# The S5 blocks' small products moved behind the dense slots of the step before, in a hybrid decoder block

## The chip, the core and the metric

The kernel runs on one core of a Trainium2 chip. The metric is the device time of one execution in microseconds; the kernel before takes 861.79 us, the median of three runs from 861.11 to 861.98. The engines are named as in the profile: PE is the tensor engine and PEld its weight loads, DVE the vector engine, ACT the scalar engine, POOL the GpSimd engine, which here only issues DMAs in the part that matters, and SP the queue that issues most loads. A product's result goes to one of eight PSUM buffers, from which DVE or ACT must copy or use it before the buffer can serve again.

## The reference

One decoder layer on 512 tokens of width 1024, with 16 meta tokens ahead of them, everything in float32. After a norm and one wide input projection, two token mixers run side by side. Then come gates, an output projection, and an MLP with squared ReLU; the change lies in the mixers.

```
# GLA: four heads, chunked linear attention with decay
scores  = where(mask, q_in @ k_in.T, 0);   o_intra = scores @ v
o_inter = q_inter @ state
state   = decay_chunk * state + k_state.T @ v
# S5: 64 groups of 16 channels, 64 complex states each
x_t = Lbar x_{t-1} + Bbar u_t ;  y_t = Re(C x_t) + D u_t
g_s = gelu(y);  glu = g_s @ w_glu + b_glu
```

## The kernel before, in words

**Dense slots.** The wide projections are cut into column blocks of 128. The list `dense` holds them in order, each with a function that takes the finished weights; `slot()` (line 761) fetches the weights of the next two entries and runs the next entry, 24 products of up to 512 columns with a split into a high and a low part (`feat_tile`, three products for each of eight depth tiles). Weights come through SP; ACT makes the high part (`whi`, line 164), DVE the low part (`wlo`, line 179), each with three buffers, so a new split starts as a slot ends. A slot takes about 5.4 us of PE. Between slots the code places the small products of the two mixers, on plain float32 operands. These places are what the change rearranges.

**Order.** In the whole stage `pinned[0]` is true: PE runs strictly in program order. ACT, DVE, POOL and SP are ordered by a planner, which takes the earliest written instruction among those that it reckons ready; after that each engine keeps to its list and waits at the head of it. In `first_block` DVE and ACT keep program order too.

**PSUM.** Four buffers (`ps_mm`, line 110) serve the dense slots, four (`ps_sm`, line 111) all the small products. `bank()` gives one of the latter; a fifth in a row waits until an earlier one has been read out.

**GLA heads** (class `Head`, line 953). `scores` (line 1054) makes products on 64 columns of the array and copies them under the causal mask into `sc` with two predicated copies on DVE (lines 1064 and 1065). `states` (line 1067) makes four states in two buffers: state 0 from the meta tokens (`kmeta`, `vmeta`, which `turn_keys` prepares with casts on ACT and subtractions on DVE), the others from `ktok` and `vtok`. `outputs`, `turn_outputs`, `turn_values` and `turn_keys` are the other places of a head; the `turn_` functions are full-width transposes.

**S5 blocks** (class `Block`, line 1110). Eight blocks of eight groups. For each block:

- `loads` fetches B and lam; `tables` (line 1124, a generator with four parts) makes M2 (lines 1130 to 1138) and M1 (lines 1140 to 1144) on DVE; `turns` (line 1147) makes the table E and loads U, eight transfers.
- `kernels` (line 1160): the kernel rows, products on 32 columns (in the profile `M,BA`), copied to `krow` and stored to `kpad`; `kernel_loads` (line 1173) reads them back shifted, eight transfers, as M3.
- `scan` (line 1180, a generator with three parts): the inputs (`U,M`, two buffers), multiplied by E on DVE and exchanged by ACT; then the scan along the chunks; then the states X.
- `output` (line 1211): the S5 output in one buffer (`M,U` and `M,X`), followed by a gelu: a square on ACT (line 1226), DVE (line 1227), a sigmoid on ACT (line 1228) and DVE (line 1230, `qt`).
- `turn_output` (line 1232): four transposes, a copy, and four stores to `qd`, from where the glu stage at the end of this part reads all blocks but the last (lines 1448 and 1450, `qi`, `gh`, `gl`).

**The steps.** `first_block` does head 0 and block 0. The loop that follows does step b for b from 1 to 7, with block b, and with head b while b is below 4. A step has five dense slots (step 7 has three): behind the first, head 0's transposes (step 2 alone), then kernel rows and inputs of block b and output of block b-1; behind the second, the outputs of the head before; behind the third, transposes of values; behind the fourth, transposes of keys and of the outputs of the head before; behind the fifth, scores and states, and last the transposes of block b-1's S5 output. Step 1 makes its inputs behind the second slot. Steps 1 to 3 hold a head's slots, step 4 four gate slots and the first r slot, step 5 five r slots, step 6 two r slots and others. Each r slot (`r_slot`, line 1252) gives DVE three more operations (lines 1260 to 1263), the first of which wait for a load of the gated head outputs (`ro`).

## Time and profile before

| what | value |
|---|---|
| median of the runs | 861.79 us (861.11 to 861.98) |
| profiled execution, its own time | 861.4 us |
| its span | 859.7 us |
| mean granted clock of PE | 0.997 |
| matmul instructions | 4952 |
| ACT whi, 128x1024 | 81 of 1059 ns |
| DVE wlo, 128x1024 | 81 of 1225 ns |
| M3 loads (M from kpad), landing | 64, 64 KB each, 2.6 us |

The profile is that of one execution. Rows of a timeline hold start and duration in microseconds, the engine, the line, the operation, the tiles written and read, the size, and how many such rows follow each other; a bracket gives the idle time of that engine before the row, and what ended it. Line 61 is the helper through which all products go, line 66 that of the transposes, so these rows are told apart by their tiles. Products on plain float32 operands are two rows each. A product row's duration holds time in which the next one runs already, so the distance between starts is what counts. In `first_block`, rows of DVE and ACT stand under line 79.

### The profile page before, as it was taken

Reading aid. Unit: us, or ns where it says so; the run is one execution under the profiler, and the core shown is the slowest. Engines: PE = TensorE matmul, PEld = TensorE weight load, DVE = VectorE, ACT = ScalarE, POOL = GpSimd, SP = SyncE. Lnnn points to the kernel's source line nnn. Section 1 sums busy time; section 2 is a strip of 40 time slices with the busy share of each in tenths; the row PEclk is TensorE's granted clock in tenths of the full one; section 3 lists DMA queues with packets and bytes.
Section 4 is the critical chain, followed back from the end, with each engine's and each line's share of the span. In section 5 each row is a group of like instructions: output and inputs, shape, how many; then the busy total and the mean of one; then the engine's idle time right before and its main releaser. Section 6 shows DMA issues by size and latency. Waiting matters only on the chain.

```text
span 859.7 us, 13744 instructions
## 1 busy us (share of the span) xinstructions
PE 849.5 (99%) x4952; PEld 726.6 (85%) x4952; DVE 680.2 (79%) x1264; ACT 465.0 (54%) x816; POOL 151.1 (18%) x265
## 2 busy tenths in 40 slices
PE   9999999999999999999999999999999999999996
PEld 8998899898988888888888889988888888888885
DVE  6999889988787499856888788667666777688886
ACT  7677466676764455335454466433222246885763
POOL 1123120140303222341121421011121100000001
PEclk9999999999999999999999999999999999999998
DMA  9887775566465856977788896498989967866564
GB/s 313 194 281 225 224 143 146 147 174 168 115 156 154 241 156 149 257 202 270 233 271 266 270 294 196 147 323 291 360 262 343 352 223 234 278 195 196 172 199 144
DMA packets 172491, 192.66 MB, mean 224 GB/s; under 512 B 18648, under 2 KB 127352, under 8 KB 172424
## 3 DMA queue, kind: packets, MB, share of 16 engines
q1 hardware_dynamic: 145040, 109.66, 45.1%
q0 software_dynamic: 25408, 77.93, 27.2%
q10 hardware_dynamic: 1976, 4.20, 1.6%
q8 instruction: 39, 0.64, 0.3%
q14 instruction: 28, 0.23, 0.1%
HBM read 149.52 MB, written 42.24 MB: 223 GB/s over the span
## 4 chain that ended last, share of the span: by engine, by line
PE 52%; issue 2%; POOL 1%; DMA 1%; DVE 1%; ACT 0%; DVEq 0%; POOLq 0%
PE mm L61 36%; PE sm L61 16%; DMA qi<-qd 1%; POOL M L1178 0%; PE sm L66 0%; POOL td L1277 0%; DVE c L1964 0%; POOL qd L1250 0%; DVE c L1938 0%; POOL qi L1448 0%; DVE gl L1450 0%; DVEq L2040 0%; ACT gh L164 0%; DMA kpad<-krow 0%; DVE ff_r L150 0%
## 5 line engine op out<-in xcount | busy, mean ns | idle before, releaser
L164 ACT ACTIVATE whi<-wraw 128x1024 fp32r<-128x1024 f32 x81 | 85.8, 1059 | 181.1 <-PE mm L61 177.6
L179 DVE TENSOR_TENSOR wlo<-wraw,whi 128x1024 fp32r<-128x1024 f32 x81 | 99.1, 1225 | 79.0 <-ACT whi L164 77.2
L61 PE MATMUL mm<-xh,whi 128*128 128x512 f32 (+2 forms) x464 | 158.5, 342 | 0.0
L61 PE MATMUL mm<-xh,wlo 128*128 128x512 f32 (+2 forms) x464 | 155.5, 335 | 0.0
L61 PE MATMUL mm<-xl,whi 128*128 128x512 f32 (+2 forms) x464 | 155.4, 335 | 0.0
L61 PE MATMUL mm<-hh,whi 128*128 128x512 f32 (+1 forms) x272 | 100.9, 371 | 0.0
L61 PE MATMUL mm<-hl,whi 128*128 128x512 f32 (+1 forms) x272 | 100.8, 371 | 0.0
L61 PE MATMUL mm<-hh,wlo 128*128 128x512 f32 (+1 forms) x272 | 100.8, 371 | 0.0
L61 PEld LDWEIGHTS mm<-xh,whi 128*128 128x128 f32 x464 | 87.4, 188 | 9.7 <-issue 1.0
L61 PEld LDWEIGHTS mm<-xh,wlo 128*128 128x128 f32 x464 | 87.4, 188 | 9.0
L61 PEld LDWEIGHTS mm<-xl,whi 128*128 128x128 f32 x464 | 87.4, 188 | 8.4
L1881 DVE TENSOR_TENSOR wlo<-wraw,whi 128x1024 fp32r<-128x1024 f32 x56 | 68.4, 1223 | 21.4 <-ACT whi L1877 21.3
L61 PE MATMUL sm<-wlo,fh 128*128 128x512 f32 x192 | 74.9, 390 | 0.0
L61 PE MATMUL sm<-whi,fl 128*128 128x512 f32 x192 | 74.8, 390 | 0.0
L61 PE MATMUL sm<-whi,fh 128*128 128x512 f32 x192 | 74.8, 389 | 0.0
L1877 ACT ACTIVATE whi<-wraw 128x1024 fp32r<-128x1024 f32 x56 | 58.7, 1050 | 15.5 <-PE mm L61 11.7
L61 PEld LDWEIGHTS mm<-hh,whi 128*128 128x128 f32 x272 | 51.3, 189 | 8.8
L61 PEld LDWEIGHTS mm<-hh,wlo 128*128 128x128 f32 x272 | 51.3, 189 | 8.7
L61 PEld LDWEIGHTS mm<-hl,whi 128*128 128x128 f32 x272 | 51.3, 189 | 8.6
L164 ACT ACTIVATE fh<-f 128x512 fp32r<-128x512 f32 x48 | 30.2, 629 | 36.8 <-PE sm L61 23.0
L61 PE MATMUL mm<-gl,whi 128*128 128x512 f32 x128 | 50.0, 390 | 0.1
L61 PE MATMUL mm<-gh,whi 128*128 128x512 f32 x128 | 49.9, 390 | 0.0
(490 smaller groups left out, 1863.2 us busy)
## 6 DMA issues: line engine op xcount, KB each, us to landing
wraw<-in_w_ff_dram SPq DMA_DIRECT2D x56, 512.0 KB, 7.5
wraw<-in_w_in_dram SPq DMA_DIRECT2D x46, 512.0 KB, 5.6
w2raw<-in_w_ff_dram POOLq DMA_DIRECT2D x16, 1024.0 KB, 9.0
t2d<-w2t POOLq DMA_DIRECT2D x16, 1024.0 KB, 6.3
wraw<-t2d SPq DMA_DIRECT2D x32, 512.0 KB, 4.2
wraw<-in_w_glu_dram SPq DMA_DIRECT2D x16, 512.0 KB, 5.2
M<-kpad POOLq DMA_DIRECT2D x64, 64.0 KB, 2.6
wraw<-in_w_o_gla_dram SPq DMA_DIRECT2D x8, 512.0 KB, 7.4
```

What stands on the lines that cost most here:

```text
L61: ins = nc.tensor.matmul(*args, **kw)
L164: return S.activation(dst, src, AF.Copy, scale=scale)
L179: V.tensor_sub(lo, raw, f32(hi))
L1877: halved = S.activation(bh, raw, AF.Copy)
L1881: V.tensor_sub(bl, raw, f32(bh))
```

## The change

The diff leaves `first_block` and the work itself as they are. It changes where the pieces stand.

- In `states`, the second product of each pair is made first, so the meta state is second.
- From block 2 on, kernel rows and inputs of block b+1 and the output of block b stand at the end of step b: in steps 1 to 3 between scores and states, from step 4 on by themselves. The kernel loads of block b+1 follow there.
- The transposes of a block's S5 output stand behind the first slot of the next step, one slot after that output; those of block 0 behind the third slot of step 1.
- Loads of B and lam come behind the first slot, tables start there too (two parts stand ahead of the fifth slot), and turns of the next block stand ahead of the fourth slot.
- Step 1 keeps kernel rows of block 1, the output of block 0 and the inputs of block 1 where they were.
- Block 7's output stands at the end of step 7, and its transposes one slot later; both come one dense slot earlier than before.

```diff
--- before.py
+++ after.py
@@ -1068,7 +1068,7 @@
             self.st = []
             for t in range(0, TT, 2):
                 pst = bank().rearrange("p (t v) -> p t v", t=2)
-                for i in range(t, t + 2):
+                for i in (t + 1, t):
                     k, v = (self.ktok[:, i - 1, :], self.vtok[:, i - 1, :]) if i else (self.kmeta, self.vmeta)
                     PE.matmul(pst[:, i % 2], k, v, start=True, stop=True)
                 for i in range(t, t + 2):
@@ -1348,29 +1348,34 @@
             continue
         this = heads[b] if b < HEADS else None
         last = heads[b - 1] if 0 < b <= HEADS else None
+        after = blocks[b + 1] if b + 1 < NBLK else None
         if b == 1:
             with tc.issue_after(heads[0].held.ins):
                 list(blk.turns())
-        following = iter(())
-        if b + 1 < NBLK:
-            following = blocks[b + 1].tables()
+        following = after.tables() if after else iter(())
         slot()
-        if b == 2:
-            heads[0].turn_outputs()
-        blk.kernels()
-        steps = blk.scan()
-        if b > 1:
+        if b == 1:
+            blk.kernels()
+            steps = blk.scan()
+            blocks[0].output()
+            blk.kernel_loads()
+        else:
+            blocks[b - 1].turn_output()
+            if b == 2:
+                heads[0].turn_outputs()
             next(steps)
-        blocks[b - 1].output()
-        blk.kernel_loads()
+            if after:
+                after.loads()
         if this:
             this.decay_load()
             with tc.issue_after(this.taken.ins), tc.issue_after(heads[0].held.ins):
                 list(this.decays())
+        if b > 1:
+            next(following, None)
         slot()
         list(steps)
-        if b + 1 < NBLK:
-            blocks[b + 1].loads()
+        if b == 1:
+            after.loads()
         if last:
             last.outputs()
         if this:
@@ -1381,14 +1386,16 @@
             slot()
         if this:
             this.turn_values()
+        if b == 1:
+            blocks[0].turn_output()
         next(following, None)
+        if after:
+            list(after.turns())
         slot()
         if this:
             this.turn_keys()
         if last and b > 1:
             last.turn_outputs()
-        if b + 1 < NBLK:
-            list(blocks[b + 1].turns())
         if b == HEADS:
             sgb.close()
             sg.close()
@@ -1396,16 +1403,21 @@
             po_ = pool("po", stack=so, padded=True)
             ogh = mk(po_, [P, KT, SEQ], F32R, tag="ogh")
             ogl = mk(po_, [P, KT, SEQ], F32R, tag="ogl")
-        next(following, None)
-        if b < NBLK - 1:
+        for _ in range(2):
+            next(following, None)
+        if after:
             slot()
         if this:
             this.scores()
+        if after:
+            after.kernels()
+            steps = after.scan()
+            next(steps)
+        blk.output()
+        if after:
+            after.kernel_loads()
+        if this:
             this.states()
-        blocks[b - 1].turn_output()
-        next(following, None)
-    slot()
-    blocks[-1].output()
     slot()
     blocks[-1].turn_output(last=True)
     while at[0] < len(dense):
```

## The prediction

> **What bounds the kernel now.** I read the first part of the page, then the waits of PE, then a table of windows over the attention and S5 stage, and then the PE rows around the places where small products stand between the dense slots.

> ```profile
> span 859.7 us, 13744 instructions
> PE 849.5 (99%) x4952; PEld 726.6 (85%) x4952; DVE 680.2 (79%) x1264; ACT 465.0 (54%) x816; POOL 151.1 (18%) x265
> ```

> ```profile
> PE sm L61 <- DVE xss L517: 1.3, 1, 1.3
> ```

> PE works from end to end: its longest wait is 1.3 us, at the start. The change adds and removes no product, only reorders them, so it can gain only what PE loses at the seams between kinds of work and in short waits that a busy PE hides. It can lose whatever PE waits for in a new place. The reserve on the other engines differs by stretch (columns of the table: stretch, its length, then busy time and instructions of PE, PEld, DVE, ACT, POOL, granted clock, DMA share, GB/s):

> ```profile
> 284.00:297.60 13.60, 13.60 (x67) 11.18 (x65) 3.79 (x5) 4.72 (x7) 4.61 (x8) 1.00 0.95 282
> 297.60:329.00 31.40, 31.40 (x205) 25.91 (x204) 29.93 (x51) 15.86 (x28) 7.19 (x13) 1.00 0.63 179
> 329.00:360.00 31.00, 30.96 (x202) 25.70 (x202) 30.28 (x50) 14.13 (x24) 7.51 (x14) 1.00 0.81 197
> ```

> At the end of step 4 (284 to 297.6) DVE is busy 3.79 of 13.6 us. In steps 5 and 6 it is busy 29.93 of 31.4 and 30.28 of 31: it is full there, and what PE wants from it earlier, it gets late.

> **Seams on PE.** Step 7's S5 place stands between two dense slots of 512 columns:

> ```profile
> 360.28 0.39 PE L61 MATMUL mm<-ogl,whi 128*128 128x512 f32 x1
> 360.50 0.39 PE L61 MATMUL mm<-ogh,wlo 128*128 128x512 f32 x1
> 360.82 0.66 PE L61 MATMUL sm<-M,BA 128*32 128x128 f32 x16
> 361.42 1.15 PE L61 MATMUL sm<-U,M 128*64 128x65 f32 x32
> 362.40 0.39 PE L61 MATMUL sm<-M,U 128*64 128x128 f32 x4
> ...
> 363.93 0.39 PE L61 MATMUL sm<-M,X 128*64 128x128 f32 x4
> 364.25 0.50 PE L61 MATMUL mm<-ogh,whi 128*128 128x512 f32 x1
> 364.59 0.40 PE L61 MATMUL mm<-ogl,whi 128*128 128x512 f32 x1
> ```

> A row starts as soon as the one before lets it, so starts are read, not durations. A dense product holds PE for 0.22 us (360.28 to 360.50). Kernel rows take 361.42 - 360.82 = 0.60, inputs 0.98, four output rows (363.93 - 362.40)/7 = 0.22, all eight groups of them 1.75. Into the place the gap is 0.32, so 0.10 is lost; the last output rows are followed after 0.32 in place of 0.22, 0.10 lost; the next gap is 0.34, 0.12 lost. So a place of products on 64 or 32 columns of the array costs 0.32 us beside its work, 0.10 on the way in and 0.22 on the way out. A place of full-width transposes loses less:

> ```profile
> 354.80 0.60 PE L66 MATMUL sm<-ident,qt 128*128 128x128 f32 x4
> 355.16 0.48 PE L61 MATMUL mm<-ogh,whi 128*128 128x512 f32 x1
> 355.47 0.40 PE L61 MATMUL mm<-ogl,whi 128*128 128x512 f32 x1
> ```

> Four transposes take 0.36, and the gap behind the next product is 0.31, 0.09 lost.

> The change joins scores and the S5 place in steps 1 to 3 (the S5 places of steps 2 to 4 go there). Each joining drops one way in and one way out, 0.32, and adds a seam from scores (64 columns) to kernel rows (32 columns), which no row shows. Its bounds are 0 and the 0.22 of a way out; I take 0.10, the way in, since that too begins narrow products. So 0.22 is saved per step, 0.7 in all (0.3 to 1.0). From step 4 on the S5 place only moves from behind the first slot to behind the last. The transposes of blocks 1 to 3, behind the states today, now stand behind the first slot: between 0 and 0.09 more each, since the states' end costs something too; I take 0.1 in all. Net gain at the seams 0.6 us.

> [...]

> **The meta state second.** In the first block the meta product waits for its operands from DVE:

> ```profile
> 130.91 0.71 DVE L79 TENSOR_TENSOR meta<-sm,meta 16x256 fp32r<-16x256 f32 x2
> 131.33 0.28 PE L61 MATMUL sm<-e_fq,e_fk 128*64 128x64 f32 x2
> 131.76 0.36 PE L61 MATMUL sm<-meta 80*128 80x256 f32 x1 [0.16 <-PE sm L61]
> ```

> ```profile
> 213.35 0.28 PE L61 MATMUL sm<-e_fq,e_fk 128*64 128x64 f32 x2
> 213.56 0.38 PE L61 MATMUL sm<-meta 80*128 80x256 f32 x1
> 213.78 1.46 PE L61 MATMUL sm<-vtok,ktok 128*128 128x256 f32 x6
> ```

> DVE ends at 131.62. From the last scores to meta it is 0.43 us, in step 2 (second fence) 0.21. So 0.22 is lost, and another state in front covers it: two of the six vtok,ktok rows, a third of 1.46. Gain 0.2; in step 2 there is no such wait, and there the swap costs nothing.

> **The last output.** Block 7's output and its transposes come one dense slot earlier, block 6's transposes two. Their way through DRAM ends just too late now:

> ```profile
> 398.82 0.39 PE L61 MATMUL mm<-gh,whi 128*128 128x512 f32 x1
> 399.27 0.50 PE L61 MATMUL mm<-gl,whi 128*128 128x512 f32 x1
> ```

> 0.45 in place of 0.22: 0.2 us lost, which the 5 us of lead removes. Behind it no row shows anything late; the dense work goes on. Gain 0.2.

> **Banks, the new wait.** The small products share four PSUM buffers (line 111). Today only step 2's first place uses more, six, with head 0's transposes ahead of S5:

> ```profile
> 180.86 1.23 PE L61 MATMUL sm<-U,M 128*64 128x65 f32 x32
> 181.97 0.44 PE L61 MATMUL sm<-M,U 128*64 128x128 f32 x4
> 182.24 0.39 PE L61 MATMUL sm<-M,X 128*64 128x128 f32 x4
> ```

> Inputs take 1.11 there in place of 0.98 and the first output rows 0.27 in place of 0.22, so 0.2 us is lost, and that goes with the change, since the place then holds three buffers of transposes alone. But the joined place uses seven: scores 1, kernel rows 1, inputs 2, output 1, states 2. So the output waits until the scores are copied out, and everything behind it on PE, states and the next dense slot, waits too.

> ```profile
> 213.46 1.22 DVE L179 TENSOR_TENSOR wlo<-wraw,whi 128x1024 fp32r<-128x1024 f32 x1 [3.56 <-ACT whi L164]
> 214.60 0.73 DVE L1064 COPY_PREDICATED sc<-tri,sm 64x512 f32<-64x512 int32 x1
> 215.35 0.45 DVE L1065 COPY_PREDICATED sc<-tri,sm 64x256 f32<-64x256 int32 x1
> ```

> ```profile
> 171.55 0.38 PE L61 MATMUL sm<-meta 80*128 80x256 f32 x1
> 174.68 0.45 DVE L1065 COPY_PREDICATED sc<-tri,sm 64x256 f32<-64x256 int32 x1
> ```

> DVE starts a weight split (wlo) as ACT finishes its part, 0.1 us before the scores are done, and the two copies follow it. In step 2 the buffer is free at 215.35 + 0.45 = 215.80; the output wants it when scores, kernel rows and inputs are through, 213.56 + 0.60 + 0.98 = 215.14. PE waits 0.65 us, and I take the same for step 3, whose pattern is the same. In step 1 DVE is behind: 174.68 + 0.45 = 175.13 against 171.55 + 1.58 = 173.13, 2.0 us; block 2's tables and turns, now due for this place, cannot fall behind the copies, work of later steps can. I take 1.2, between step 2's 0.65 and 2.0 and nearer the first, since that queue is the usual one. Sum 2.5 us (2.0 to 3.3). The states' two buffers are those of kernel rows and first inputs; their copies follow the scores' by under 1 us, while the output products take 1.75, which hides them. If DVE is later than that, it costs so much again.

> [...]

> **Covered moves.** Loads of B and lam, the eight U loads, kernel row stores and the eight M3 loads move on SP's and POOL's queues with their blocks; kernel loads keep a whole step (about 31 us) before use, U gains, since output frees its buffer a slot earlier. Nothing if the order within the queues holds; DMA share is already 0.95 in 284 to 297.6, so a late weight there could cost PE some tenths. Sigmoids of S5 now stand beside those of the gate slot, which drops table loads on ACT; PE does not wait for ACT there, so 0.

> **Sum.** -0.6 at the seams, -0.2 for meta, -0.2 for the last output, -0.2 in step 2's first place, +2.5 for the banks: +1.3 us. The profiled execution took 861.4 (span 859.7 and 1.7 around it), the median is 861.8; I carry the difference over: 861.8 + 1.3 = 863.1.

> **Rivals.**

> (a) *DVE's full stretch makes PE wait, slower.* Block 6's inputs need its table, and turned outputs need the gelu chain.

> ```profile
> 297.62 0.69 DVE L1261 TENSOR_TENSOR rs<-rs,ro 128x512 f32<-128x512 f32 x1 [3.02 <-DMA ro<-og]
> 300.83 0.39 PE L61 MATMUL sm<-M,X 128*64 128x128 f32 x4
> 306.23 0.69 DVE L1230 TENSOR_TENSOR qt<-q,sm 128x512 f32<-128x512 f32 x1 [0.46 <-ACT q L1228]
> 329.32 0.70 DVE L1144 TENSOR_TENSOR M<-M,B 128x512 f32<-128x512 f32 x1
> 329.70 0.88 PE L61 MATMUL sm<-U,M 128*64 128x65 f32 x12
> ```

> The chain from output to qt took 306.92 - 301.05 = 5.9 us in step 5. Today four slots cover it; then one slot, 24 x 0.22 to 0.23, 5.4. Block 6's table ends at 330.02, 0.3 after its inputs start; it falls due a slot earlier. DVE also stands 3.02 us for a load that S5 work queued behind it shares. For it: the full DVE rows. Against: S5 work of block 5 moves into the idle stretch before 297.6 and eases what follows, and PE's own waits give time back. It decides once DVE is more than a slot behind the place. Price 0.5, the difference, for each of blocks 4 to 6, and up to 3 at the table: with the sum, +2.8 to +5.8, 864.6 to 867.6; middle 866.1.

> (b) *The scores are copied first or fast, no bank wait.* Then the 2.5 falls away: -1.2, 860.6. For it: 0.1 us decides whether wlo or the copies go first on DVE. Against: the order held at step 2, and step 1 is late anyway.

> (c) *The gains are larger.* Everything above at its good end, with the 0.3 us at 329.70 also gone: -1.0 - 0.2 - 0.2 - 0.2 - 0.3 = -1.9, 859.9. It needs no new wait anywhere.

> **How the numbers follow.** A measurement of this kernel can tell about 0.2%, 1.7 us, from no change. Forecast 0.45, (a) 0.28, (b) 0.20, (c) 0.07. Slower by more than that: (a), and near a third of the forecast, whose sum stands 0.4 from the edge, 0.42 in all. Faster: most of (c), 0.05. The rest, 0.53, is within. The range reaches from 860.1, under (b), to 866.5 in (a); about 2 in 10 lie outside. The likeliest case is therefore a small loss that hardly shows.

> **What would show it.** Right: in steps 1 to 3 a PE gap of 0.6 to 1.3 us ahead of the first M,U row behind the inputs, released by the predicated copy; no gap at 131.76 and none at the first gl product of block 6; a place fewer per step. Wrong: no such gap (then b), or gaps of over 0.5 us ahead of qt transposes or inputs after 290 us (then a).

## The result and the profile after

| | before | after |
|---|---|---|
| median of the runs | 861.88 us (861.11 to 863.19, 6 runs) | 866.43 us (864.60 to 869.46, 6 runs) |
| ratio of the times, with its interval | | 1.0059 (1.0048 to 1.0070) |
| profiled execution, its own time | 861.40 us | 869.46 us |

The changed kernel is slower by 0.5 to 0.7%, on the side that the prediction gave 0.42. Its median lies at the upper end of the range of 860.1 to 866.5 and 3.3 us above the predicted time. The times also lie farther apart than before. The profiled execution is the slowest of the six, so the page and the account below are those of a slow one.

The page and the waits of PE after (columns: who waited for what, us in total, times, longest):

```profile
span 867.6 us, 13734 instructions
PE 852.4 (98%) x4952; PEld 728.6 (84%) x4952; DVE 681.2 (79%) x1264; ACT 460.8 (53%) x812; POOL 150.9 (17%) x265
```

```profile
PE sm L66 <- DVE e_gk L1023: 2.1, 1, 2.1
PE sm L66 <- ACT vtok L979: 2.0, 1, 2.0
PE sm L61 <- DVE xss L517: 1.3, 1, 1.3
PE sm L61 <- PE sm L61: 1.1, 2, 0.6
```

The wait for `xss` was there before. The top two are new, and the prediction names neither. The two of 0.6, whose releaser the profile does not find, are the joined places of steps 2 and 3, which it does name.

**First stall, step 1, third place.** PE's rows, then ACT's:

```profile
158.58 1.03 PE L66 MATMUL sm<-ident,vt 128*128 128x128 f32 x8
161.58 0.86 PE L66 MATMUL sm<-ident,qt 128*128 128x128 f32 x4 [1.97 <-ACT vtok L979]
162.67 0.63 PE L61 MATMUL mm<-xl,whi 128*128 128x512 f32 x1
163.10 0.63 PE L61 MATMUL mm<-xh,wlo 128*128 128x512 f32 x1
```

```profile
160.94 1.08 ACT L979 COPY vtok<-sm 128x512 f32<-128x512 f32 x2
165.34 1.57 ACT L1098 ACTIVATE on<-sm,ors 128x256 f32<-128x256 f32 x4 [2.27 <-DVE ors L161]
```

Head 0's outputs, made in the place before, hold two of the four small buffers until ACT has written `on`, from 165.34 us. The value transposes fill the other two. Block 0's transposes (`qt`), which the change put behind them, are the fifth, and PE stands until ACT has copied `vtok`. Then the dense products start 0.43 us apart (162.67 to 163.10) where 0.22 to 0.23 is usual.

**Second stall, step 2, fourth place.** DVE's order, first after, then before:

```profile
210.72 0.69 DVE L999 TENSOR_TENSOR d<-b 128x512 f32<-128x512 f32 x1 [7.28 <-DMA b<-bd]
211.47 0.70 DVE L1023 TENSOR_TENSOR e_gk<-kT,e_gk 128x528 f32<-128x528 f32 x1
```

```profile
203.41 0.70 DVE L1023 TENSOR_TENSOR e_gk<-kT,e_gk 128x528 f32<-128x528 f32 x1
204.97 0.69 DVE L999 TENSOR_TENSOR d<-b 128x512 f32<-128x512 f32 x1
```

Line 999 is the first decay product of head 3, line 1023 the key product of head 2. With the places shifted, the planner listed the first ahead of the second. DVE keeps to its list, so it stands 7.28 us for a transfer that nobody needs yet, and the key product stands behind it:

```profile
209.79 0.38 PE L66 MATMUL sm<-ident,vt 128*16 128x128 f32 x2
212.22 0.60 PE L66 MATMUL sm<-ident,e_gk 128*16 128x128 f32 x4 [2.05 <-DVE e_gk L1023]
```

**The clock behind both.** Windows over the two stalls (columns: stretch, its length, busy time and instructions of PE, PEld, DVE, ACT, POOL, granted clock, DMA share, GB/s):

```profile
158.48:161.89 3.41, 1.44 (x14) 1.20 (x13) 3.35 (x7) 3.26 (x7) 0.00 (x0) 1.00 0.86 210
161.89:165.30 3.41, 3.41 (x12) 2.74 (x10) 3.41 (x17) 0.71 (x2) 1.94 (x4) 0.50 0.14 34
209.68:213.09 3.41, 1.36 (x12) 0.96 (x10) 2.37 (x6) 1.60 (x3) 0.00 (x0) 1.00 0.01 4
213.09:216.50 3.41, 3.41 (x12) 2.85 (x11) 3.37 (x7) 2.19 (x5) 1.08 (x2) 0.50 0.25 61
```

Behind each stand the granted clock is 0.50 for 3.41 us, which loses an estimated 3.41 / 2 = 1.7 us more.

**What was foreseen.** In step 2's joined place PE stands ahead of the first output rows:

```profile
222.40 1.16 PE L61 MATMUL sm<-U,M 128*64 128x65 f32 x32
224.13 0.44 PE L61 MATMUL sm<-M,U 128*64 128x128 f32 x4 [0.57 <-PE sm L61]
```

```profile
223.58 0.44 DVE L1065 COPY_PREDICATED sc<-tri,sm 64x256 f32<-64x256 int32 x1
```

Inputs take 0.98, so 224.13 - 222.40 - 0.98 = 0.75 us is lost, and the same in step 3. The second copy of the scores ends at 223.58 + 0.44 = 224.02, just ahead of PE's next start, as foreseen. The wait ahead of the meta product is gone, and the first glu products of block 6 are 0.22 apart:

```profile
132.33 0.28 PE L61 MATMUL sm<-e_fq,e_fk 128*64 128x64 f32 x2
132.54 0.70 PE L61 MATMUL sm<-vtok,ktok 128*128 128x256 f32 x2
132.89 0.47 PE L61 MATMUL sm<-meta 80*128 80x256 f32 x1
...
407.35 0.39 PE L61 MATMUL mm<-gh,whi 128*128 128x512 f32 x1
407.57 0.39 PE L61 MATMUL mm<-gl,whi 128*128 128x512 f32 x1
```

**Account of the profiled pair.** Stands 1.97 + 2.05, clock 2 x 1.7, joined places 2 x 0.75: 8.9 us. The difference is 869.46 - 861.40 = 8.06, of which 1.0 arose ahead of the changed code (the first kernel rows start at 105.40 in place of 104.40). So 7.1 remains, and the gains are about 1.8.

### The profile page after: what moved, and what is told of

It reads as the page before. It is cut to its first block, busy times and chain, and to the rows that moved or that the text cites. A ratio compares the mean times of both kernels' runs of the same rounds, so it can differ in the third digit from the quotient of the medians.

```text
span 867.6 us, 13734 instructions
## 1 busy us (share of the span) xinstructions
PE 852.4 (98%) x4952; PEld 728.6 (84%) x4952; DVE 681.2 (79%) x1264; ACT 460.8 (53%) x812; POOL 150.9 (17%) x265
## 4 chain that ended last, share of the span: by engine, by line
PE 85%; DVE 6%; DMA 4%; ACT 2%; issue 1%; SPq 1%; ACTq 0%; DVEq 0%
PE mm L61 63%; PE sm L61 20%; DMA wraw<-in_w_in_dram 2%; PE sm L66 1%; DMA b<-bd 1%; DMA xt<-in_x_dram 1%; DVE wlo L179 1%; SPq L492 0%; DVE wlo L79 0%; DVE M L1133 0%; DVE c L1976 0%; ACT whi L79 0%; DVE xT L79 0%; DVE st L79 0%; DVE epb L240 0%
## 5 line engine op out<-in xcount | busy, mean ns | idle before, releaser
L164 ACT ACTIVATE whi<-wraw 128x1024 fp32r<-128x1024 f32 x81 | 85.9, 1060 | 182.5 <-PE mm L61 175.6
L179 DVE TENSOR_TENSOR wlo<-wraw,whi 128x1024 fp32r<-128x1024 f32 x81 | 98.8, 1221 | 78.5 <-ACT whi L164 75.4
L61 PE MATMUL mm<-xh,whi 128*128 128x512 f32 (+2 forms) x464 | 159.6, 344 | 0.0
L61 PE MATMUL mm<-xh,wlo 128*128 128x512 f32 (+2 forms) x464 | 156.0, 336 | 0.0
L61 PE MATMUL mm<-xl,whi 128*128 128x512 f32 (+2 forms) x464 | 156.0, 336 | 0.0
L61 PE MATMUL mm<-hh,whi 128*128 128x512 f32 (+1 forms) x272 | 100.8, 371 | 0.0
L61 PE MATMUL mm<-hl,whi 128*128 128x512 f32 (+1 forms) x272 | 100.7, 370 | 0.0
L61 PE MATMUL mm<-hh,wlo 128*128 128x512 f32 (+1 forms) x272 | 100.7, 370 | 0.0
L61 PEld LDWEIGHTS mm<-xh,whi 128*128 128x128 f32 x464 | 88.1, 190 | 9.5 <-issue 0.5
L61 PEld LDWEIGHTS mm<-xh,wlo 128*128 128x128 f32 x464 | 87.9, 189 | 9.3
L61 PEld LDWEIGHTS mm<-xl,whi 128*128 128x128 f32 x464 | 88.0, 190 | 8.7
L61 PE MATMUL sm<-wlo,fh 128*128 128x512 f32 x192 | 74.8, 390 | 0.0
L61 PE MATMUL sm<-whi,fh 128*128 128x512 f32 x192 | 74.7, 389 | 0.0
L61 PE MATMUL sm<-whi,fl 128*128 128x512 f32 x192 | 74.7, 389 | 0.0
L61 PEld LDWEIGHTS mm<-hh,whi 128*128 128x128 f32 x272 | 51.2, 188 | 8.8
L61 PEld LDWEIGHTS mm<-hh,wlo 128*128 128x128 f32 x272 | 51.2, 188 | 8.7
L61 PEld LDWEIGHTS mm<-hl,whi 128*128 128x128 f32 x272 | 51.2, 188 | 8.7
L61 PE MATMUL mm<-gh,whi 128*128 128x512 f32 x128 | 49.8, 389 | 0.0
L61 PE MATMUL mm<-gl,whi 128*128 128x512 f32 x128 | 49.8, 389 | 0.0
L61 PE MATMUL mm<-gh,wlo 128*128 128x512 f32 x128 | 49.8, 389 | 0.0
```

Of the source, the lines that this page charges most:

```text
L61: ins = nc.tensor.matmul(*args, **kw)
L164: return S.activation(dst, src, AF.Copy, scale=scale)
L179: V.tensor_sub(lo, raw, f32(hi))
```

## The experiments

Theory: two stalls cost most of it, each a stand of PE with half a clock behind it. Rival 1: the joined places carry it, as predicted. Rival 2: another engine is simply behind, and a wait that is removed turns up elsewhere. Twelve runs follow, eleven edited kernels and the changed kernel again. Where a ratio stands, it is against the kernel before in the same measurement, whose medians were 861.30 to 861.62 us.

### The two stalls, one by one

**Block 0's transposes a place later.**

```diff
-        if b == 1:
-            blocks[0].turn_output()
         next(following, None)
...
             this.turn_keys()
+        if b == 1:
+            blocks[0].turn_output()
```

> The changed kernel with one thing moved: block 0's output is transposed one place later, behind the key transposes of step 1, so that the third place of step 1 needs no fifth bank. Theory (two stalls, each followed by dense products at half clock): the 2.0 us wait for the vtok copy goes, and the half clock behind it (granted clock 0.50 from 163 to 165 us), 1.8 us, goes with it, 3.8 us faster than the changed kernel; the third place costs 0.9 beside its work in place of 5.1, the fourth 1.1 in place of 0.7. Rival 1 (the seven banks of the joined places carry the loss, as the prediction had it): under 0.5 us. Rival 2 (ScalarE is behind, the wait only moves): the key transposes of step 1 wait instead, and 2 us or less is won.

Measured: 863.25 us, ratio 1.0018 (1.0009 to 1.0026). The first stall and the half clock are gone (the profiled execution's mean clock is 0.998), and so was, in that execution, the second. But less than 3.8 us was won (3.2 against the first measurement of the change, 1.7 against the second, at the end), for new waits:

```profile
PE sm L61 <- issue: 1.3, 1, 1.3
PE sm L61 <- PE sm L61: 1.2, 2, 0.6
PE sm L66 <- ACT on L1098: 0.5, 1, 0.5
```

The first is the joined place of step 1, where PE now comes 3 us earlier (its output rows start 174.85 - 172.45 - 0.98 = 1.4 us late); in the changed kernel the stall before it had given DVE and ACT the time, and there was no wait. The third is the place that the transposes moved to. Another 0.3 us stands ahead of the `qt` transposes of step 6. So the theory holds for the stall, and rival 2 for a part of what it cost.

**Decay products behind the key products.**

```diff
-            V.tensor_mul(self.kx, kT[...], self.kx)
+            self.keyed = V.tensor_mul(self.kx, kT[...], self.kx)
...
-            with tc.issue_after(this.taken.ins), tc.issue_after(heads[0].held.ins):
+            with tc.issue_after(this.taken.ins), tc.issue_after((last.keyed if b > 2 else heads[0].held).ins):
                 list(this.decays())
```

> The changed kernel with one order on VectorE put back: from step 3 on a head's decay products stand behind the key products of the head before, as they did before the change. Theory: the 7.3 us stand of VectorE for the transfer into b no longer holds up the key products, PE's 2.05 us wait ahead of the key transposes of step 2 and the half clock behind it go, up to 3.8 us in an execution like the profiled one and some 2 us at the median, and the times lie closer together than 864.6 to 869.5; the fourth place of step 2 costs 1.6 in place of 5.4. Rival 1 (the transfer's late landing itself decides): VectorE stands as long behind the key products and holds up weight splits and query products, PE waits at the scores of step 2, and the time stays within 0.5 us. Rival 2 (only the joined places matter): no change in the time.

Measured: 863.70 us, ratio 1.0031 (1.0019 to 1.0043), the times from 863.14 to 865.25. DVE's rows:

```profile
203.69 0.71 DVE L1023 TENSOR_TENSOR e_gk<-kT,e_gk 128x528 f32<-128x528 f32 x1 [1.92 <-ACT kT L1022]
...
208.06 0.69 DVE L999 TENSOR_TENSOR d<-b 128x512 f32<-128x512 f32 x1 [1.58 <-DMA b<-bd]
```

The key product no longer waits for the transfer, and PE's wait for `e_gk` is gone; its wait of 2.0 us for `vtok` and the half clock behind that (0.50 from 160.50 to 161.00) stand as before. DVE still stands 1.58 us for the transfer, but in this profile nothing that PE waits for is listed behind it, which speaks against rival 1.

**Both**: the two edits above together.

> Both repairs together, block 0's transposes behind the key transposes and the decay products behind the key products. Theory: what is left of the change is two bank waits of 0.8 us against gains of about 2 us at seams and covered waits: 861 us, 0 to 1 us below the kernel before. Rival (joined places carry the loss): 865 to 866 us.

Measured: 863.85 us, ratio 1.0026 (1.0017 to 1.0036). Neither: the repairs do not add. This profile has the 1.3 us of step 1's joined place, 0.6 in the other two, 0.5 for `on`, and 0.7 ahead of the `qt` transposes of step 6. One reason why this came out no faster than the first repair alone is in the profile of that one: it had no wait for `e_gk` that the second repair could remove. Whether that holds for its other executions is not shown.

**Work put into the wait.**

```diff
         if b == 1:
+            fill = bank("mm")
+            for _ in range(9):
+                PE.matmul(fill, xh[:, 0, NM : NM + P], xh[:, 0, NM:], start=True, stop=True)
             blocks[0].turn_output()
```

> The changed kernel with work added: nine products of 512 columns, read by nobody, stand on TensorE between the vt transposes and block 0's transposes in the third place of step 1, in a bank of the dense products, where TensorE waits 2.0 us now. Theory (TensorE's clock drops because it stands still): the wait is filled, the clock stays at 1.00 from 162 to 166 us, and the time falls by 1.8 us although nine products more are computed. Rival (the clock drops for another reason, such as the load that all engines draw): the dense products behind it start 0.43 us apart as before, and the time stays or rises by up to 0.2 us.

Measured: 865.16 us, ratio 1.0044 (1.0031 to 1.0056). PE's rows and the windows:

```profile
158.53 2.33 PE L61 MATMUL mm<-xh 128*128 128x512 f32 x9
160.75 0.66 PE L66 MATMUL sm<-ident,qt 128*128 128x128 f32 x4
```

```profile
155.99:159.41 3.42, 3.42 (x28) 3.29 (x27) 3.36 (x7) 2.61 (x5) 0.00 (x0) 1.00 1.10 237
159.41:162.82 3.41, 3.41 (x18) 2.65 (x17) 3.41 (x14) 2.37 (x5) 0.49 (x1) 1.00 0.17 43
```

The transposes stand as late as before, and the clock stays at 1.00. This does not yet show that the half clock comes from PE standing still. The last section finds, from the beginnings of the half clock, that the clock changes on a grid of stretches of 3.41 us. In this execution a boundary of the grid, reckoned from the half clock at its end, lies at 159.41, inside the wait that was filled (158.77 to 160.75). Left empty, it would have taken an estimated 0.64 us from one stretch and 1.34 from the next, and in no profile does the clock halve behind a stretch with that little idle time: the seven of the last section have 3.41 - 1.57 = 1.84 us or more. Neither expectation holds as a whole: the clock stayed up, but the 1.8 us do not show in the time, which is 1.3 us below the first measurement of the change and 0.2 above the second. The joined place of step 1 then waits 1.15 us, as in the first repair.

### The joined places

**Kernel rows in a dense bank**, on top of the transposes a place later:

```diff
         def kernels(self):
 
-            ps = bank()
+            ps = bank("mm")
```

> The first repair (block 0's transposes one place later, 863.25 us) with one more bank: the kernel rows of S5 go to a bank of the dense products, so that the joined places of steps 1 to 3 use six of the small banks in place of seven and the output need not wait for the copies of the scores. Theory (bank waits): the joined places, 7.6, 6.9 and 6.9 us beside their work in that kernel, all come to 6.15, 3.1 us faster, 860.2. Rival 1 (VectorE is full in steps 5 and 6): TensorE comes there 3 us earlier and stands longer for the gelu chain (0.5 us in the first repair), 861 to 862. Rival 2 (the dense products miss the bank): a wait of the next dense slot's products for a bank, and the time stays within 0.5 us of 863.25.

Measured: 863.69 us, ratio 1.0023 (1.0012 to 1.0033). The waits of the joined places are gone from the list but for 0.2 us, yet nothing is won:

```profile
PE sm L66 <- ACT on L1098: 1.5, 2, 1.1
PE sm L66 <- DVE e_gk L1023: 1.4, 1, 1.4
...
PE sm L61 <- ACT vs L1188: 0.2, 1, 0.2
```

This kernel still has head 3's decay products ahead of head 2's key products, and with PE early the second stall is back (DVE stands 5.1 us for `b` here). None of the three expectations had that.

**All repairs**: kernel rows in a dense bank, decay products behind key products, and block 0's transposes where the change put them, in a dense bank too:

```diff
-            ps = bank()
+            ps = bank("mm" if self.blk == 0 else "sm")
             for i in range(4):
                 PE.transpose(ps[:, i * P : (i + 1) * P], ...)
```

> The changed kernel, its order on TensorE as it is, with three repairs: kernel rows and the transposes of block 0 in banks of the dense products, and the decay products behind the key products from step 3 on. Theory: no bank wait and no stop of VectorE is left, and the gains of the change stand alone: meta 0.2, joined places and transposes 0.4, block 6's place 0.4, the last output 0.6, in all 1.6 below the kernel before, 859.8 us. Rival (VectorE is full in steps 5 and 6): TensorE waits ahead of the gelu chain's transposes for 0.5 to 1.1 us, 860.3 to 860.9. Rival (the losses lie elsewhere): 863 us or more.

Measured: 860.85 us (860.35 to 861.82, 11 runs), ratio 0.9989 (0.9980 to 0.9998): just below the kernel before. PE's waits in this profile, behind the first block:

```profile
PE sm L61 <- ACT vs L1188: 0.6, 1, 0.6
PE sm L61 <- DVE sc L1065: 0.3, 1, 0.3
```

Both stand in step 1's joined place, ahead of the states. The theory's 859.8 left them out: 859.8 + 0.9 = 860.7. The first rival's range, 860.3 to 860.9, holds the median too, but the wait that it names, ahead of the gelu chain's transposes, is not in the profile.

**Kernel rows and inputs ahead of the scores**, on top of both first repairs:

```diff
-        if this:
-            this.scores()
         if after:
             after.kernels()
             steps = after.scan()
             next(steps)
+        if this:
+            this.scores()
         blk.output()
```

> Both first repairs (863.85 us) with another order in the joined places: kernel rows and inputs ahead of the scores, so that the output takes the bank of the kernel rows, copied earlier, and not that of the scores. Theory (the wait is for the copies of the scores alone): 3.1 us faster, 860.8. Rival (VectorE and ScalarE are behind with all copies of the place, so that output or states wait as long for another bank): within 0.5 us of 863.85.

Measured: 864.22 us, ratio 1.0027 (1.0016 to 1.0037). The rival holds. In place of the scores' copies PE waits in all three joined places for ACT's exchange of the inputs:

```profile
PE sm L61 <- ACT vs L1188: 3.8, 3, 1.5
```

Seven uses of four buffers made PE wait in both orders that were tried; a buffer more took most of the wait away.

### The rest of the change alone

**S5 in its new places from the end of step 4 on**; steps 1 to 3 keep S5 where it was (cut to its core):

```diff
-        if b == 1:
+        if b <= 4:
+            if b == 2:
+                heads[0].turn_outputs()
             blk.kernels()
             steps = blk.scan()
-            blocks[0].output()
+            if b > 1:
+                next(steps)
+            blocks[b - 1].output()
             blk.kernel_loads()
...
-        if after:
+        if after and b >= 4:
             after.kernels()
```

> The change without its joined places: steps 1 to 3 keep S5 where it was, and S5 moves to its new places from the end of step 4 on; the meta product second and the output a place later stay as in the change. Theory (the loss lies wholly in steps 1 to 3, the gains after them are real): meta 0.2, block 6's place 0.4 and the last output 0.6 below the kernel before, 860.2 us. Rival (a of the prediction, VectorE full in steps 5 and 6): TensorE waits ahead of the transposes of blocks 4 to 6, 0.5 to 1.1 us for each, and the time is at or above that of before, 861.4 to 863.

Measured: 863.32 us, ratio 1.0022 (1.0013 to 1.0031). Rival (a) of the prediction, at one place in place of three and, in the profiled execution (864.01 us), at more than its price. PE, DVE and the windows:

```profile
302.81 0.66 PE L66 MATMUL sm<-ident,qt 128*128 128x128 f32 x4 [1.88 <-DVE qt L1230]
```

```profile
297.71 0.69 DVE L1261 TENSOR_TENSOR rs<-rs,ro 128x512 f32<-128x512 f32 x1 [2.98 <-DMA ro<-og]
...
302.06 0.69 DVE L1230 TENSOR_TENSOR qt<-q,sm 128x512 f32<-128x512 f32 x1 [0.48 <-ACT q L1228]
```

```profile
299.91:303.32 3.41, 1.53 (x10) 1.03 (x9) 2.93 (x5) 3.33 (x8) 0.00 (x0) 1.00 0.64 123
303.32:306.74 3.42, 3.42 (x11) 2.65 (x10) 3.42 (x6) 1.05 (x3) 3.02 (x6) 0.50 0.66 149
```

DVE stands 2.98 us for the load of the gated outputs, with the gelu chain of block 4 behind it on its list. One slot does not cover that: PE stands 1.88 us and loses 1.7 more to the clock. Eight of the eleven executions have a mean clock of 0.997 or 0.998, so the half clock is hardly the rule here. The stand alone leaves 1.2 of the 3.1 us by which the median misses the theory's 860.2, and where they are lost is open. In the changed kernel and with all repairs DVE does not stand there for that load, and the transposes of step 5 come without a wait.

### All repairs less one, and the change again

**Kernel rows back in a small bank.**

```diff
         def kernels(self):
 
-            ps = bank("mm")
+            ps = bank()
```

> All repairs (860.85 us) without one: the kernel rows of S5 stand in a small bank again, as in the change, so the joined places need seven. Theory: TensorE waits for the scores' copies 1.5 us in step 1 and 0.8 in steps 2 and 3, against 0.9 in step 1 alone with the bank, so 2.2 us slower, 863.0. Rival (with the other stalls gone the copies come in time): within 0.5 us of 860.85.

Measured: 864.30 us, ratio 1.0033 (1.0020 to 1.0046). In the profiled execution, the fastest of five at 862.86, the first joined place waits 1.98 us, the others as in the changed kernel:

```profile
175.30 0.44 PE L61 MATMUL sm<-M,U 128*64 128x128 f32 x4 [1.98 <-issue]
```

So the joined places are worth 2 us or more once nothing hides them. The median is 1.4 us above this execution, and 1.3 above the theory's 863.0. Behind this stand the clock stays at 1.00. Two of the slower executions, 864.30 and 864.77, have a mean clock of 0.996 and 0.995, which fits a half clock there. The slowest, 865.37, has 0.997 and stays open.

**Decay products free again.**

```diff
-            with tc.issue_after(this.taken.ins), tc.issue_after((last.keyed if b > 2 else heads[0].held).ins):
+            with tc.issue_after(this.taken.ins), tc.issue_after(heads[0].held.ins):
```

> All repairs (860.85 us) without one: head 3's decay products stand ahead of head 2's key products on VectorE again, as in the change. Theory: VectorE stands for the transfer into b, PE waits ahead of the key transposes of step 2, 1.4 us and, with what it pulls behind it, up to 4.0 as in the profile of the rows in a dense bank; 862 to 865, and the times spread over 2 us or more, since the landing of the transfer decides. Rival (the transfer lands in time once the places before it are fast): within 0.5 us of 860.85.

Measured: 864.93 us, ratio 1.0035 (1.0023 to 1.0047), the times from 862.52 to 865.76. As the theory had it: PE waits 1.4 us for `e_gk`, and the clock is 0.50 for 3.42 us behind it, from 209.07. The way is longer here: DVE stands 4.5 us for `b` ahead of a step of `ors`, so ACT's `on` and, listed behind it, the copy of `kT` that the key product reads come late.

**Block 0's transposes back in a small bank.**

```diff
         def turn_output(self, last=False):
 
-            ps = bank("mm" if self.blk == 0 else "sm")
+            ps = bank()
```

> All repairs (860.85 us) without one: block 0's transposes stand in a small bank again, the fifth of the third place of step 1. Theory: 2.0 us wait and half clock behind it, the place costs 5.2 us in place of 1.35, of which the joined place of step 1 gives 0.9 back, since TensorE comes there later: 2.9 us slower, 863.8. Rival (the half clock comes from elsewhere): 2 us slower or less.

Measured: 862.86 us, ratio 1.0013 (1.0004 to 1.0022), 2.0 us above all repairs. The rival's size, but the theory's mechanism: in the profiled execution (862.98 us) the wait is there, and the clock is 0.50 for one stretch of 3.41 us behind it:

```profile
157.92:161.33 3.41, 1.43 (x11) 1.16 (x10) 3.41 (x8) 3.02 (x7) 0.00 (x0) 1.00 0.95 194
161.33:164.74 3.41, 3.41 (x9) 2.69 (x9) 3.41 (x15) 0.94 (x3) 2.43 (x4) 0.50 0.25 59
```

Step 1's joined place then waits for nothing, so 2.0 + 1.7 - 0.9 = 2.8 us is due, and the two profiled executions differ by 862.98 - 860.51 = 2.5. The median is lower because the half clock seems to come in only a part of the executions: four have a mean clock of 0.997 or 0.998 and take 861.79 to 862.16 us, the other seven have 0.995 or 0.996 and take 862.78 to 863.79.

**The changed kernel again**, without an edit.

> The changed kernel itself once more, for a second profile and more times. Theory: the stall of step 1 (5.1 us in the third place) stands in every execution, that of step 2 varies with the landing of the transfer into b and makes the spread; median 865 to 867. Rival (both stalls are fixed): the second profile shows 5.4 us in the fourth place of step 2 again.

Measured: 864.94 us, ratio 1.0042 (1.0030 to 1.0054), just under the 865 to 867 that the theory gave. In its profile the first stall is the same (2.0 us), the second shorter:

```profile
PE sm L66 <- ACT vtok L979: 2.0, 1, 2.0
PE sm L66 <- DVE e_gk L1023: 1.4, 1, 1.4
```

Behind the second the clock stays at 1.00. DVE stands 6.6 us for `b` in place of 7.28. That agrees with a second stall that depends on a landing; two profiles do not prove it.

The spread of the times has another cause beside it. Of the fourteen profiles, those with a mean clock of 0.998 have no half clock while PE works, and those with 0.996 or less have one or two; 0.997 occurs with and without one. Of the eleven executions of the changed kernel, six have 0.998 and take 864.35 to 866.27 us, and five have 0.995 or 0.996 and take 865.98 to 869.46. So the half clock seems to come in about half of the executions, while the first stall is 2.0 us in both profiles; the last section shows why that can be.

## Why the prediction was wrong, point by point

The sum was +1.3 us and the measured difference is 866.43 - 861.88 = 4.55. The gains came out, and the loss was larger than priced, by three steps.

- **Seams, meta, last output** (-0.6, -0.2, -0.2): right as a sum; the gains were not measured one by one. The seam from scores to kernel rows, taken as 0.10 us, is 176.44 - 176.23 - 0.12 = 0.09 in step 1 of the profile after. The waits are gone in the profile after, and with all repairs the kernel is 0.8 us below the one before although 0.9 us of waits are left, so the gains are about 1.7. That is a little more than the 1.2 summed with step 2's first place: the inputs of block 6 no longer wait for their table, the 0.3 us that only rival (c) counted.
- **Banks, the new wait, where it was put** (+2.5 for the joined places): right in place and mechanism. Two of the three terms measure 0.75 where 0.65 stood; step 1's 1.2 was 0 in the changed kernel, because the stall ahead of it let the other engines catch up, and 1.4 without that stall. In sum 1.5 in the changed kernel, 2.9 in the first repair.
- **Banks, the count of places**: the first step that failed. The prediction counted the buffers of one place at a time and held the joined place for the only one with more than four. It priced the new place of the transposes of blocks 1 to 3, at 0 to 0.09 us each, and has no term for those of block 0. But head 0's outputs carry two buffers over from the place before, so step 1's third place has five, and PE stands 1.97 us there.
- **Covered moves** ("nothing if the order within the queues holds"): the second. The order on the queues was looked at as far as the transfers go; the order on DVE is set by the planner too, and it changed. An instruction that can wait for a transfer came ahead of one that PE needed: 7.28 us on DVE, 2.05 on PE.
- **A wait priced at its length**: the third. In the profiled execution two stands of 2 us cost 3.7 us each. By their mean clock about half of the executions have no half clock; there the first two steps alone are the miss. No row of the profile before shows PE standing so long in this stage, so there was none to price it by.
- **Rival (a)**: did not happen in the change; the gaps of over 0.5 us that it asked for after 290 us are absent. Its mechanism is real, as the kernel with S5 moved from step 4 on shows.

One wait kept the next from showing. That fits with the three repairs being worth 3.5, 4.1 and 2.0 us when each is taken from the full set, but 5.6 us together (866.43 to 860.85), or 4.1 against the second measurement of the change.

## What to carry to other kernels

Count buffers over neighbouring places, with what the place before still holds, and not only within the place that is edited. When a planner orders an engine, look after a move at which instruction can stand for a transfer, and what is listed behind it. A removed wait paid here only as far as the next engine was ready (863.85 us with two repairs, 860.85 with all), so repair all known stalls together before judging one. Where a stall can bring a half clock or not, as here, look at the mean clock of every execution (0.995 to 0.998 in the changed kernel) before reading a difference of 1 or 2 us.

## What the hardware showed

The half clock was not expected. While PE works it appears seven times, in six profiles, and lasts 3.41 or 3.42 us each time, whatever PE had waited for. In the changed kernel its two beginnings, 161.89 and 213.09, are 51.20 us apart, 15 stretches of 51.20 / 15 = 3.413 us. The clock also halves in every profile once PE is done, in the kernel before at 854.78, in the changed kernel at 865.03, 703.14 us or 206.0 times 3.413 behind the first. So the beginnings fall on a grid in these traces, and the one at the end gives the grid also where the clock held until then. That tells why a stand of 1.98 us did not halve it, with the kernel rows back in a small bank:

```profile
170.40:173.82 3.42, 2.92 (x73) 2.44 (x72) 3.41 (x5) 3.04 (x4) 0.21 (x1) 1.00 0.10 36
173.82:177.23 3.41, 1.93 (x33) 1.79 (x33) 3.37 (x10) 1.23 (x4) 0.90 (x2) 1.00 0.67 151
856.49:859.90 3.41, 0.00 (x0) 0.00 (x0) 0.77 (x2) 0.00 (x0) 0.00 (x0) 0.50 0.60 185
```

The end's beginning, 856.49, is 682.67 us or 200.0 times 3.413 behind 173.82. The stand, 173.32 to 175.30, lies across that boundary, so each stretch keeps 1.93 us of PE's work or more. With the rows in a dense bank, two stands of 1.08 and 1.36 us (up to 207.71 and 209.45) are parted likewise, by a boundary at 207.80, reckoned from that execution's end. In the second profile of the change the stand of 1.4 us, wherever it falls, leaves an estimated 3.41 - 1.4 = 2.0 us of work or more in a stretch.
